# Where a decoder trunk computes its adaLN modulation columns: other quotas for its stages

## The chip, the cores and the metric

The kernel runs on one core of one Trainium2 chip. The metric is the device time of one execution in microseconds. One core has five engines that run their own queues: TensorE (matrix products, here PE; its weight loads are PEld), VectorE (DVE), ScalarE (ACT), GpSimd (POOL) and SyncE (SP), which issues every load of this kernel. Data lies in SBUF, products accumulate in PSUM.

## What is computed

A decoder trunk of four layers over 256 positions and 1,024 features, batch 1. Each layer is a SwiGLU, a token mixer and a second SwiGLU; the mixers are RWKV-7, Mamba-2, sliding-window attention and RWKV-7 again. Each of the twelve sub-layers normalises its input and modulates it by shift, scale and gate vectors that depend on one conditioning vector c:

```python
c_act = jax.nn.silu(c)
for i in range(DEPTH):
    mod = (c_act @ ada_w[i] + ada_b[i]).reshape(bsz, N_SUB, 3, d)
    shift, scale, gate = mod[:, :, 0], mod[:, :, 1], mod[:, :, 2]
    h = adaln(x, norm_g[i, 0], shift[:, 0], scale[:, 0])
    x = x + MACARON_W * gate[:, 0, None] * swiglu(h, ffn_w_in[i, 0], ffn_w_out[i, 0])
    h = adaln(x, norm_g[i, 1], shift[:, 1], scale[:, 1])
    ...
    x = x + gate[:, 1, None] * y
    h = adaln(x, norm_g[i, 2], shift[:, 2], scale[:, 2])
    x = x + MACARON_W * gate[:, 2, None] * swiglu(h, ffn_w_in[i, 1], ffn_w_out[i, 1])
return x
```

The line left out is the mixer. What matters here is the first line of the loop: `c_act @ ada_w[i]` is a vector times a matrix of 1,024 by 9,216 float32 numbers for each layer. None of it depends on x, so it can be computed at any time before the sub-layer that uses it.

## The kernel before

Activations are held transposed, features on the 128 partitions, in eight blocks of 128 x 256. Every dense product is float32 made of three passes on TensorE: a weight tile of 128 x 1,024 floats (512 KB) is loaded by `unit` (lines 292 to 305), ScalarE rounds it to its high half (`whi`, line 299), VectorE subtracts to get the low half (`wlo`, line 303), and then come high x high, high x low and low x high (lines 328 to 330, or 520 to 522 for an output projection). One weight tile is 24 products of 128x128 by 128x256. A SwiGLU has 66 such tiles: 44 of its first matrix, and 22 of its second, whose products are interleaved with the first's as its inputs come.

**Modulation columns.** The modulation is cut into 288 columns of 128 numbers: 72 a layer, 24 a sub-layer (eight pairs of scale and shift, then eight gates). `mod_step` (lines 247 to 262) takes the next of a fixed list, loads its 512 KB of `ada_w` into a buffer named `ada`, and lets VectorE multiply it by c and sum along the row in one instruction (line 253); a small instruction (257 or 261) finishes a scale or a gate. The buffer comes from the same ring of four that the raw weight tiles use (`wp`, tag `raw`), and the load is issued by SP in the order of its queue, between the weight loads.

**Who calls it.** Four mechanisms decide where a column is made:

- A plan (`mod_plan`, 275): a quota of columns spread over a number of weight tiles. After each tile's low half, `mod_tick` (285, called at 304) adds the rate to a credit and makes a column for each whole one, until the quota is used up. A SwiGLU sets its plan from `QUOTA` over 0.8 x 66 = 52.8 tiles (655), so that its last tiles are free of columns; Mamba sets 8 over 48 (871). At the end of either the rate is set to 0, and RWKV and attention set no plan.
- `mod_some(n, upto)` (280): makes up to n columns now, as long as fewer than `upto` have been made in all. RWKV calls it in its recurrence (1561, queued on VectorE behind the end of the triangular inverse), after it beside the bonus terms (1574) and the head reads (1580), and in its output loop `outputs` (1456).
- `mod_until` (264): makes all that is still missing up to a place in the list. It is called where a column is needed: before the residual addition for the gates (545), and in `u_open` or `rw_open` for the scale and shift of the next sub-layer (479, 1053). If enough columns have been made before, it does nothing.
- The first SwiGLU makes its own 16 before it starts.

**The order of the engines.** The code is traced, and the framework puts each engine's instructions into a fixed queue by their dependences and its own estimate of times; `issue_after` pins some behind others. On the chip each engine works through its queue in that order, so an instruction that waits holds up those behind it. At the end of a sub-layer, `out_proj` prefetches up to three weight tiles of the next one, opens its modulation, and then, for each of the eight blocks, finishes the products, adds to x (`x_add`, line 608) and prepares the next input (`u_part`, 490 and 491).

**RWKV.** The stage runs dense products for k, v and r through a queue of pieces (`dense_queue`, `fill`), between which the steps of the decay, the triangular inverse and the recurrence are placed, then `read_heads`, a normalisation for the first four heads (`norm(0)`), the loop `outputs(0, ...)`, a normalisation for the last four heads (`norm(1)`, whose steps are lines 580 to 593 on VectorE, 1081 and 844 on TensorE) and `outputs(1, ...)`. Each turn of the loop gates and splits one block and feeds it to the output projection, which loads one tile of `rwo`.

Of the kernel before, what the change touches and what calls it, by code (L numbers as in the profile page):

```python
# [21 lines left out]
S = 256  # L22
DEPTH = 4

QUOTA = ((24, 28), (28, 28), (28, 24), (24, 0))
DFF = 2816
NJ = D // P
NF = DFF // P
# [155 lines left out]
class Trunk:  # L184
# [465 lines left out]
    def ffn(self, i, s):  # L650
        nc = self.nc
        self.phase(f"ffn{i}{s}")
        with ExitStack() as ctx:
            self.weights(ctx, 7)
            self.mod_plan(QUOTA[i][s // 2], 0.8 * 3 * NF)
            gp1 = ctx.enter_context(self.tc.tile_pool(name="gp1", bufs=1))
# [190 lines left out]
    def mb(self, i, k):  # L847
# [4 lines left out]
        with ExitStack() as ctx:  # L852
# [15 lines left out]
                v.memset(t[:, 0:3], 0.0)  # L868
            tri2 = self.c("tri")[:, None, :].to_broadcast([P, 2, P])

            self.mod_plan(8, 48)
            for g in range(8):
                chans, zs = [], []

# [194 lines left out]
    def rw(self, i, k):  # L1069
# [1 line left out]
        self.phase(f"rw{i}")  # L1071
        v, act = nc.vector, nc.scalar
        hold = [False]
        ahead = 84 if i == 0 else 72 * DEPTH

        def mm(*a, **k):
            ins = nc.tensor.matmul(*a, **k)  # L1077
            self.last = ins.ins if hold[0] else None
# [12 lines left out]
        with ExitStack() as ctx:  # L1091
# [54 lines left out]
            def flat(t):  # L1146
                return t.rearrange("p k c -> p (k c)")
# [271 lines left out]
            def read_heads(g, jj):  # L1419

                s, uv, mr, ys, sn = ss[g], uvs[g], mrs[g], yss[g], sns[:, 16 * g : 16 * g + 16]
                o = self.bank("mm", S)
                for c in range(4):
                    for par, p in enumerate(half):
                        x = o[p, c * 64 : c * 64 + 64]
                        mm(x, uv[:, par, jj, c], mr[:, par, 4 * jj + c], start=True, stop=c == 0)
                        if c:
                            mm(x, s[c - 1][p, jj], er[g][p, jj, c, 1:], start=False, stop=True)
                act.copy(ys[:, jj], o)
                sq = sp.tile([P, S], F32, tag="sq", name="sq")  # L1430
                act.activation(sq, o, AF.Square)
                for b in range(2):
                    mm(sn[:, b * 8 + 2 * jj : b * 8 + 2 * jj + 2], sq[:, b * P : b * P + P], self.c("b2"),
                       start=True, stop=True)
# [6 lines left out]
            def outputs(g, yt, g2, mid):  # L1441
                ys = yss[g]
                oh, ol = (pool.tile([P, 4, S], F32R, tag=f"{t}{g}", name="o") for t in ("b", "e"))
                for jj in range(4):
                    j = 4 * g + jj
                    y = ys[:, jj]
                    rb = self.bank("aux", S)
                    self.heads(rb, 2 * jj, yt)
                    v.scalar_tensor_tensor(y, y, self.v(f"lnw{k}", j), rb, ALU.mult, ALU.mult)
                    v.scalar_tensor_tensor(y, y, self.v(f"lnb{k}", j), kx[g][:, jj], ALU.add, ALU.add)  # L1450
                    o = self.bank("aux", S)
                    mm(o, flat(g2)[:, j * P : j * P + P], sg, start=True, stop=False)
                    mm(o, flat(mid)[0:32, j * P : j * P + P], hm[0:32], start=False, stop=True)
                    v.tensor_tensor(y, y, o, ALU.mult)
                    self.split(oh[:, jj], ol[:, jj], y)
                    self.mod_some(2, ahead)
                    feed(oh[:, jj], ol[:, jj])
                    yield 1

# [66 lines left out]
            def one_by_one(*gens):  # L1526
                gens = list(gens)
                while gens:
                    for x in list(gens):
                        if next(x, 0) == 0:  # L1530
                            gens.remove(x)
                        else:
                            yield
# [22 lines left out]
            more = inner(1, bd)  # L1556
            for n, _ in enumerate(one_by_one(chain(0), chain(1))):
                self.fill()
                if n in range(1, 24, 3):
                    with self.tc.issue_after(self.inv_end):  # L1560
                        self.mod_some(1, ahead)
                if n in (17, 20, 22):
                    self.drain(3 - (17, 20, 22).index(n))
                    next(more)
# [12 lines left out]
            yss[1] = slot("f1", [4, S], "ys")  # L1577
            for jj in range(4):
                read_heads(1, jj)
                self.mod_some(2, ahead)  # L1580
                self.fill(3)
            hold[0] = False
            for _ in outputs(0, yt, g2, mid):
                pass
            for _ in outputs(1, norm(1), g2, mid):
                pass
# [35 lines left out]
```

## Time and profile before

| | |
|---|---|
| three executions | 2573.45, 2555.08 and 2565.6 us; median 2565.6 |
| the profiled execution | 2566.54 us, its span 2564.4 us |
| TensorE clock granted over it | 0.95 of full speed |
| data moved | 521.98 MB, on average 204 GB/s |
| loads of `ada_w` | 288 of 512 KB, median 4.4 us from issue to landing |

The page's strips over 40 slices of 64 us show how the stages differ:

```profile
PE   6999999889999989999999999899999999999999
DVE  7876785788787788988788877997787766866854
PEclk9999997699999998999999999999999998886999
GB/s 312 288 260 154 100 87 145 191 186 298 285 191 293 283 136 123 157 176 186 300 284 190 302 279 155 154 219 290 258 185 295 261 103 74 84 152 179 203 195 128
```

Each digit is the busy share of a slice in tenths, PEclk the granted clock in tenths. TensorE is busy almost throughout. The slices near 300 GB/s are SwiGLUs; those near 100 are RWKV. [...]

### The profile page before, as it was taken

The page shows a single profiled execution, that of the slowest core. Times are in us where ns is not written, and L with a number is a line of the kernel's source. Part 1 is how long each engine was busy: PE and PEld are TensorE (multiplying, and loading weights), DVE is VectorE, ACT ScalarE, POOL GpSimd, SP SyncE. Part 2 cuts the span into 40 slices and gives each one's busy share as a digit, 9 for nine tenths or more (in the row PEclk, how much of TensorE's full clock was granted, in tenths as well). Part 3 has the DMA queues.
Part 4 walks back from the last instruction along what each step waited for, and adds up shares of the span by engine and source line. Part 5 has one row for each costly group of instructions (what it writes and reads, how often), then busy time and mean ns, then how long its engine had stood idle before and what let it go on. Part 6 is the DMA issues. An engine that isn't in the chain of part 4 may idle for free.

```text
span 2564.4 us, 51852 instructions
## 1 busy us (share of the span) xinstructions
PE 2447.3 (95%) x20868; PEld 2280.3 (89%) x20868; DVE 1985.6 (77%) x4181; ACT 1262.2 (49%) x2261; POOL 8.1 (0%) x14
## 2 busy tenths in 40 slices
PE   6999999889999989999999999899999999999999
PEld 5998877689999988999999999799999987777999
DVE  7876785788787788988788877997787766866854
ACT  3446661254454456765445445554454464612643
POOL 0000000000000000000000000000000000000000
PEclk9999997699999998999999999999999998886999
DMA  8874224558858843455885884468758732245663
GB/s 312 288 260 154 100 87 145 191 186 298 285 191 293 283 136 123 157 176 186 300 284 190 302 279 155 154 219 290 258 185 295 261 103 74 84 152 179 203 195 128
DMA packets 145392, 521.98 MB, mean 204 GB/s; under 512 B 16128, under 2 KB 19456, under 8 KB 145024
## 3 DMA queue, kind: packets, MB, share of 16 engines
q1 hardware_dynamic: 145152, 518.67, 60.5%
q8 instruction: 164, 2.69, 0.4%
q14 instruction: 76, 0.62, 0.1%
HBM read 516.50 MB, written 2.10 MB: 202 GB/s over the span
## 4 chain that ended last, share of the span: by engine, by line
PE 55%; DMA 19%; DVE 15%; ACT 5%; issue 4%; ACTq 0%; SPq 0%; DVEq 0%
DMA raw<-ffn 11%; PE aux L1077 8%; DMA ada<-ada_w 7%; PE aux L330 5%; DVE wlo L303 5%; PE aux L328 5%; PE aux L329 5%; PE mm L328 4%; PE mm L329 4%; PE mm L330 4%; PE mm L521 4%; PE mm L520 4%; PE mm L522 4%; ACT whi L299 3%; DVE ada L253 3%
## 5 line engine op out<-in xcount | busy, mean ns | idle before, releaser
L299 ACT CAST whi<-raw 128x1024 fp32r<-128x1024 f32 x671 | 700.1, 1050 | 678.3 <-DMA raw<-ffn 464.8
L303 DVE TENSOR_TENSOR wlo<-raw,whi 128x1024 fp32r<-128x1024 f32 x671 | 817.4, 1222 | 232.1 <-ACT whi L299 225.6
L328 PE MATMUL aux<-hh,whi 128*128 128x256 f32 x2576 | 722.7, 281 | 12.9 <-DVE ft L676 9.8
L330 PE MATMUL aux<-hh,wlo 128*128 128x256 f32 x2576 | 721.4, 280 | 13.3 <-DVE wlo L303 13.2
L329 PE MATMUL aux<-hl,whi 128*128 128x256 f32 x2576 | 719.9, 279 | 0.0
L328 PEld LDWEIGHTS aux<-hh,whi 128*128 128x128 f32 x2576 | 487.1, 189 | 17.8 <-DVE ft L676 12.2
L330 PEld LDWEIGHTS aux<-hh,wlo 128*128 128x128 f32 x2576 | 486.5, 189 | 15.9 <-DVE wlo L303 15.9
L329 PEld LDWEIGHTS aux<-hl,whi 128*128 128x128 f32 x2576 | 489.0, 190 | 0.0
L253 DVE CUSTOM_DVE_ANT_0 ada<-ada,cb,vec 128x1024 f32<-128x1024 f32 x288 | 368.6, 1280 | 88.2 <-DMA ada<-ada_w 88.0
L520 PE MATMUL mm<-gh,whi 128*128 128x256 f32 x1408 | 392.6, 280 | 9.3 <-ACT gh L678 9.3
L522 PE MATMUL mm<-gh,wlo 128*128 128x256 f32 x1408 | 390.4, 280 | 3.3 <-DVE wlo L303 3.1
L521 PE MATMUL mm<-gl,whi 128*128 128x256 f32 x1408 | 392.5, 280 | 0.4
L328 PE MATMUL mm<-hh,whi 128*128 128x256 f32 (+1 forms) x1056 | 313.5, 303 | 13.5 <-ACT cy L885 5.1
L329 PE MATMUL mm<-hl,whi 128*128 128x256 f32 (+1 forms) x1056 | 308.3, 294 | 0.4
L330 PE MATMUL mm<-hh,wlo 128*128 128x256 f32 (+1 forms) x1056 | 307.6, 294 | 0.0
L520 PEld LDWEIGHTS mm<-gh,whi 128*128 128x128 f32 x1408 | 266.1, 189 | 10.9 <-ACT gh L678 10.9
L521 PEld LDWEIGHTS mm<-gl,whi 128*128 128x128 f32 x1408 | 267.0, 190 | 1.8 <-DVE gl L679 1.8
L522 PEld LDWEIGHTS mm<-gh,wlo 128*128 128x128 f32 x1408 | 264.7, 189 | 4.2 <-DVE wlo L303 4.2
L328 PEld LDWEIGHTS mm<-hh,whi 128*128 128x128 f32 x1056 | 205.2, 197 | 28.3 <-issue 7.2
L329 PEld LDWEIGHTS mm<-hl,whi 128*128 128x128 f32 x1056 | 207.6, 197 | 9.1 <-issue 2.5
L330 PEld LDWEIGHTS mm<-hh,wlo 128*128 128x128 f32 x1056 | 207.6, 197 | 5.9 <-issue 4.3
L678 ACT ACTIVATE gh<-ft 128x256 fp32r<-128x256 f32 x176 | 72.9, 415 | 153.1 <-DVE ft L677 152.1
(357 smaller groups left out, 3087.7 us busy)
## 6 DMA issues: line engine op xcount, KB each, us to landing
raw<-ffn SPq DMA_DIRECT2D x522, 512.0 KB, 4.6
ada<-ada_w SPq DMA_DIRECT2D x288, 512.0 KB, 4.4
raw<-rkv SPq DMA_DIRECT2D x48, 512.0 KB, 3.5
raw<-mbin SPq DMA_DIRECT2D x48, 512.0 KB, 3.4
raw<-rwo SPq DMA_DIRECT2D x16, 512.0 KB, 4.5
raw<-mbout SPq DMA_DIRECT2D x16, 512.0 KB, 3.3
lora<-lora SPq DMA_DIRECT2D x12, 512.0 KB, 3.8
raw<-qkv SPq DMA_DIRECT2D x12, 512.0 KB, 4.4
```

Of the source, the lines that this page charges most:

```text
L253: nc.vector.tensor_tensor_reduce(out=raw, in0=raw, in1=self.cb, scale=1.0, scalar=self.v("ada_b", i * 72 + col), op0=ALU.mult, op1=ALU.add ...
L299: nc.scalar.copy(hi[:, :n], raw[:, :n])
L303: nc.vector.tensor_tensor(lo[:, :n], raw[:, :n], hi[:, :n].bitcast(F32), ALU.subtract)
L328: mm(out, hi, xh, start=start, stop=False)
L329: mm(out, hi, xl, start=False, stop=False)
L330: mm(out, lo, xh, start=False, stop=stop)
L520: mm(o, hi, xh, start=k == 0 and j % 2 == 0, stop=False, skip_group_check=True)
L521: mm(o, hi, xl, start=False, stop=False, skip_group_check=True)
L522: mm(o, lo, xh, start=False, stop=k == n - 1 and j % 2 == 1, skip_group_check=True)
L678: nc.scalar.activation(gh, t, AF.Copy, scale=0.5)
L1077: ins = nc.tensor.matmul(*a, **k)
```

## The change

The quotas, two limits and a few calls change; no arithmetic does. All 288 columns are made as before, from the same data with the same instructions, but in other places.

```diff
-QUOTA = ((24, 28), (28, 28), (28, 24), (24, 0))
+QUOTA = ((24, 30), (30, 30), (30, 30), (28, 8))
...
-            self.mod_plan(8, 48)
+            self.mod_plan(14, 48)
...
-        ahead = 84 if i == 0 else 72 * DEPTH
+        ahead = 70 if i == 0 else 280
+        self.mod_plan(10 if i == 0 else 6, 24)
...
                     self.split(oh[:, jj], ol[:, jj], y)
-                    self.mod_some(2, ahead)
                     feed(oh[:, jj], ol[:, jj])
...
-                if n in range(1, 24, 3):
+                if n in range(1, 24, 2 if i == 0 else 3):
                     with self.tc.issue_after(self.inv_end):
                         self.mod_some(1, ahead)
...
                 read_heads(1, jj)
-                self.mod_some(2, ahead)
+                self.mod_some(1, ahead)
                 self.fill(3)
```

In order: the quota of each SwiGLU (first and second of the four layers), Mamba's plan, the limit of `mod_some` in the two RWKV stages and a plan for their dense tiles, which had none, the call in RWKV's output loop taken out, twelve calls instead of eight in the recurrence of layer 0, and one column instead of two at each of the four head reads.

## The prediction

> **What bounds the kernel now.** I read the page first, then the busy times in windows cut at the sub-layers, then the waits and timeline where TensorE stands still.
>
> ```profile
> span 2564.4 us, 51852 instructions
> PE 2447.3 (95%) x20868; PEld 2280.3 (89%) x20868; DVE 1985.6 (77%) x4181; ACT 1262.2 (49%) x2261; POOL 8.1 (0%) x14
> PE 55%; DMA 19%; DVE 15%; ACT 5%; issue 4%; ACTq 0%; SPq 0%; DVEq 0%
> L253 DVE CUSTOM_DVE_ANT_0 ada<-ada,cb,vec 128x1024 f32<-128x1024 f32 x288 | 368.6, 1280 | 88.2 <-DMA ada<-ada_w 88.0
> ```
>
> TensorE is busy for 95% of the span, and the chain that ended last runs more on it than on all else. A modulation column is one 512 KB load and 1.28 us of VectorE; there are 288 before and after. The change moves columns only, so the question is what a column costs in each place. The windows below are the sub-layers: RWKV of layer 0, SwiGLU, SwiGLU, Mamba, SwiGLU, SwiGLU, attention, SwiGLU, SwiGLU, RWKV of layer 3, last SwiGLU.
>
> ```profile
> core 0: us, PE busy (x) PEld busy (x) DVE busy (x) ACT busy (x) POOL busy (x), PEclk, DMA share, GB/s
> 226.50:532.30 305.80, 289.99 (x2744) 233.12 (x2743) 217.57 (x550) 139.98 (x301) 3.50 (x5) 0.84 0.39 130
> 532.30:729.40 197.10, 190.87 (x1602) 189.27 (x1602) 160.87 (x285) 96.47 (x145) 0.00 (x0) 0.99 0.76 254
> 729.40:922.80 193.40, 186.19 (x1595) 183.59 (x1593) 157.54 (x278) 94.96 (x142) 0.00 (x0) 1.00 0.76 254
> 922.80:1176.00 253.20, 246.84 (x1925) 228.48 (x1924) 217.30 (x540) 163.42 (x374) 0.00 (x0) 0.96 0.46 150
> 1176.00:1370.80 194.80, 191.35 (x1601) 189.40 (x1600) 159.36 (x284) 97.19 (x146) 0.00 (x0) 0.99 0.76 254
> 1370.80:1566.40 195.60, 187.42 (x1592) 184.65 (x1592) 158.01 (x281) 94.23 (x142) 0.00 (x0) 0.99 0.76 254
> 1566.40:1677.30 110.90, 97.00 (x751) 87.56 (x750) 101.03 (x398) 60.76 (x164) 0.00 (x0) 0.92 0.47 158
> 1677.30:1869.00 191.70, 187.24 (x1594) 185.83 (x1592) 152.71 (x268) 95.57 (x142) 0.00 (x0) 1.00 0.76 249
> 1869.00:2061.90 192.90, 188.78 (x1580) 187.57 (x1579) 151.96 (x262) 93.82 (x140) 0.45 (x1) 0.99 0.74 247
> 2061.90:2379.00 317.10, 302.45 (x2786) 238.87 (x2785) 220.28 (x564) 141.14 (x301) 3.52 (x5) 0.84 0.36 119
> 2379.00:2564.40 185.40, 180.26 (x1574) 179.46 (x1572) 118.51 (x191) 86.72 (x128) 0.00 (x0) 1.00 0.55 177
> ```
>
> The first column is the stage's time, the second TensorE's. Attention idles most for its length (14 us of 111); both RWKV stages have a granted clock of 0.84. The columns in seven of the same windows:
>
> ```profile
> 226.50:532.30 305.80, 45.95 (x36) 0.84 0.39 130
> 532.30:729.40 197.10, 35.87 (x28) 0.99 0.76 254
> 922.80:1176.00 253.20, 8.97 (x7) 0.96 0.46 150
> 1566.40:1677.30 110.90, 16.51 (x13) 0.92 0.47 158
> 1677.30:1869.00 191.70, 30.77 (x24) 1.00 0.76 249
> 2061.90:2379.00 317.10, 40.91 (x32) 0.84 0.36 119
> 2379.00:2564.40 185.40, 0.00 (x0) 1.00 0.55 177
> ```
>
> **Counting the columns.** The order of columns is fixed, so running the new quotas through the code gives the new places. Three SwiGLU quotas of 28 that follow each other, and a fourth, become 30 (8 columns more in all); 24 becomes 30 behind attention (6) and 28 ahead of the last RWKV (4). Mamba has 46 of its 48 planned loads inside the plan, so 14/48 gives 13 instead of 7 (6). Attention has no quota: it makes whatever is missing up to column 208 in one burst. It starts with 195 and needs 13 now; it will start with 203 and need 5. RWKV 0 goes from 36 to 30: some 7 beside the dense products, 13 in the recurrence instead of 8, 8 instead of 12 after it, 2 in the output loop instead of 16. RWKV 3 goes from 32 to 15: about 5 beside dense products, 8 in the recurrence as before, and the limit of 280 leaves one or two after it. The last SwiGLU makes 7. So 31 columns leave attention (8) and RWKV (6, 17), and 25 go to SwiGLUs and 6 to Mamba.
>
> **Attention: -10.** Here the burst stands between the residual additions, in VectorE's queue, while TensorE's next products are queued behind the additions and wait for them.
>
> ```profile
> L253 DVE CUSTOM_DVE_ANT_0 ada<-ada,cb,vec 128x1024 f32<-128x1024 f32 x10 | 12.7, 1283 | 1.3 <-DMA ada<-ada_w 1.3
> L520 PE MATMUL mm<-oh,whi 128*128 128x256 f32 x12 | 5.3, 445 | 10.6 <-DVE x L608 10.6
> 1656.00:1676.00 20.00, 9.38 (x47) 8.60 (x46) 18.66 (x45) 5.18 (x14) 0.00 (x0) 0.66 0.83 293
> ```
>
> These are the groups and the window of 1656 to 1676: ten columns (12.7 us), 10.6 us of idle TensorE behind them, and a clock of 0.66, so that 2 x 0.34 x 20 = 13.6 us went by at half speed with TensorE half busy. Eight columns fewer leave five. Three of the 13 ran before 1656, so by the old times two of the five remain, 2.6 us: 10.6 - 2.6 = 8 us of waiting goes, and I estimate 2 us of the slow products. Late next are those two. Bounds: -6 (the five stand where the ten stood, half the wait stays) to -13 (all of it, with the clock).
>
> **The output loops: -13.** In RWKV 0 TensorE runs through its first four heads' output without a break, then waits for the second normalisation, whose short VectorE steps are queued between columns. In RWKV 3 the same place waits less:
>
> ```profile
> 499.96 0.38 PE L1081 MATMUL aux<-con,ry 128*8 128x128 f32 x2 [2.79 <-DVE ry L593]
> 502.05 0.58 PE L844 MATMUL aux<-yth,hot 8*128 8x256 f32 x1 [1.70 <-ACT yth L835]
> ```
>
> ```profile
> 2348.69 0.38 PE L1081 MATMUL aux<-con,ry 128*8 128x128 f32 x2 [0.93 <-DVE ry L593]
> 2350.18 0.41 PE L844 MATMUL aux<-yth,hot 8*128 8x256 f32 x1 [1.11 <-ACT yth L835]
> ```
>
> ```profile
> 502.00:526.00 24.00, 22.95 (x108) 18.04 (x108) 17.29 (x33) 5.72 (x8) 0.00 (x0) 0.68 0.57 188
> 2348.00:2373.00 25.00, 23.20 (x116) 18.08 (x116) 14.18 (x31) 8.13 (x14) 0.00 (x0) 0.73 0.40 138
> ```
>
> The waits are 4.5 and 2.0 us; without columns the steps are ready while TensorE still works on the first four heads, and I count 4 and 1.5 us as gone. What follows is bound by TensorE (22.95 of 24 us, 23.20 of 25) at clocks of 0.68 and 0.73: 2 x 0.32 x 24 = 15.4 and 2 x 0.27 x 25 = 13.5 us at half speed, worth 7.7 and 6.7 us if the clock stayed up. I take half, 7.2, as the stages' mean of 0.84 shows that the clock falls elsewhere too: 4 + 1.5 + 7.2, about 13. Bounds 0 (the rwo load or its split is late instead) to 21. [...]
>
> The four columns fewer in the head reads of each stage count nothing: TensorE works without a break there.
>
> **Columns beside the dense products and in the recurrence: +5.** Seventeen new places (7 and 5, and 4 or 5 in RWKV 3), and each puts a load into SP's queue and the ring of four raw buffers that it shares with the weights, and 1.28 us into VectorE's queue, behind which stand the chain's own steps and the next weight's split; TensorE waits for those. POOL's fills wait for none of it.
>
> ```profile
> 290.00:320.00 30.00, 30.00 (x353) 25.57 (x351) 23.58 (x68) 20.69 (x48) 0.95 (x1) 0.96 0.29 98
> 400.00:420.00 20.00, 18.59 (x260) 15.21 (x259) 13.68 (x34) 3.89 (x9) 0.00 (x0) 1.00 0.49 159
> ```
>
> In the first window (dense products) TensorE never stops and DMA is at 0.29, in the second (recurrence, with six columns in 20 us) it stops for 1.4 us. So the cover is the dense queue. Bounds 0 and 17 x 1.28 = 22; I take 0.3 us each, near the row with six columns and 1.4 us.
>
> **Mamba: +2.** Six columns, 7.7 us of VectorE, in a stage where it is busy for 217 of 253 us and TensorE for 247. Bounds 0 and 7.7; a quarter, since TensorE's queue covers most.
>
> **SwiGLUs: +12.** With 24 columns they took 191.7 and 192.9, with 28 they took 193.4, 194.8 and 195.6 (leaving out 197.1, which begins behind RWKV): 2.3 us for 4 columns, 0.58 each. The last took 185.4 with none, so from none to 24 a column is 0.29. New: 8 + 6 + 4 = 18 at 0.58 is 10.4, and 7 at 0.29 is 2.0. The bounds come from these windows inside the SwiGLUs, and the last one from a stretch where TensorE has run out of weights:
>
> ```profile
> 1230.00:1290.00 60.00, 60.00 (x512) 60.00 (x511) 47.91 (x72) 27.04 (x34) 0.00 (x0) 1.00 0.89 301
> 2420.00:2480.00 60.00, 60.00 (x532) 60.00 (x531) 37.53 (x47) 29.12 (x39) 0.00 (x0) 1.00 0.68 220
> 842.00:882.00 40.00, 36.62 (x305) 35.71 (x305) 29.36 (x48) 17.43 (x24) 0.00 (x0) 1.00 0.83 277
> ```
>
> TensorE has two rhythms without any idle time: 60/512 = 117 ns a product and 60/532 = 113. A weight tile is 24 products, 2.81 or 2.71 us, and a quota of 30 in 52.8 tiles asks for 1.568 loads of 0.524 MB in it: 293 GB/s in the slow rhythm, 304 in the fast. The loads reach 301. So in the slow rhythm 18 columns cost nothing (bound 0), in the fast one they make TensorE wait, as at 842, at 0.524/301 = 1.74 us a load (bound 18 x 1.74 = 31). I take the difference between the stages, which lies between. [...]
>
> **Sum.** -10 - 13 + 5 + 2 + 12 = -4 (rounded from -3.6) against the profiled execution of 2566.5 us, whose span is 2564.4: 2563 us. That execution is 1 us above the median of the three runs, 2565.6. A measurement of this kernel tells about 1% (26 us) from no change; the three runs alone are 18 us apart.
>
> **The rivals.**
>
> *The loads become the bound (slower).* Place: the seven SwiGLUs. Price: 1.74 us for each of 25 columns, 43.5 instead of 12.4. It decides once TensorE is in the fast rhythm, 304 asked against 301 reached. Time: 2563 + 31 = 2594. For it: the waits at 842. Against it: the slow rhythm covers, and the last SwiGLU has DMA at 0.68.
>
> *The SwiGLUs cover their columns and the clock stays up (faster).* Place: 502 to 526 and 2348 to 2373, and the SwiGLUs in the slow rhythm. Output loops -20, attention -13, SwiGLUs +2, Mamba and dense products +5: -26, 2540. For it: at 28 columns 512 products in 60 us with no idle time. Against it: the stages with 28 are longer than those with 24. [...]
>
> *The change doesn't do what it says.* If the list scheduling leaves the remaining attention columns and output-loop loads where they block now, both gains halve: 2563 + 11 = 2574.
>
> *The rhythm.* 66 x 24 = 1,584 products a SwiGLU at 4.4 ns is 7 us, and each pause of TensorE seems to choose anew; eight SwiGLUs can shift the time by some 10 us either way without any reason in the change.
>
> **How the numbers follow.** Forecast and its neighbourhood 0.60, covered and warm 0.17, loads the bound 0.09, gains halved 0.14. Faster than 2540: most of the second, 0.17. Slower than 2591: most of the third, 0.08. Within 1%: 0.75. The range takes in attention's and the loops' bounds on one side and the loads' on the other, without their ends: 2534 to 2590.
>
> **What would show it.** Right: 5 columns in attention and TensorE's idle time before its last products under 4 us; attention near 101 us; no wait of 2.8 us for the second normalisation; SwiGLUs of 193 to 198 us; a last SwiGLU of 186 to 189. Wrong: idle TensorE in the SwiGLUs above 10 us each with SP waiting for VectorE, new waits in RWKV before its recurrence, or a granted clock in RWKV under 0.84.

## The result and the profile after

The changed kernel takes 2584.7 us (median of seven executions, 2578.9 to 2599.4) against 2565.6 us for the kernel before (seven, 2554.4 to 2573.5): a ratio of 1.0101, with a 95% interval of 1.0071 to 1.0130. The time lies in the range of 2534 to 2590, because that range took in a bound for slower loads; the forecast itself was 4 us less, and the kernel became 19 us slower. The profiled execution took 2583.94 us, 17.4 more than that of before. Its page begins so:

```profile
span 2582.2 us, 51802 instructions
PE 2435.1 (94%) x20868; PEld 2265.3 (88%) x20868; DVE 1983.3 (77%) x4181; ACT 1261.5 (49%) x2261; POOL 8.1 (0%) x14
PE 41%; DMA 27%; DVE 19%; ACT 7%; issue 5%; ACTq 0%; SPq 0%; DVEq 0%
```

The chain that ended last tells it first: TensorE's share fell from 55% to 41%, the loads' rose from 19% to 27% and VectorE's from 15% to 19%. TensorE is busy for 12 us less in a span that is 18 us longer, so 30 us of new idle time stand in it. The windows by sub-layer say where (columns as before: stage, its time, TensorE and its products, weight loads, VectorE, ScalarE, POOL, clock, DMA share, GB/s):

```profile
0.00:235.30 235.30, 198.13 (x1548) 191.32 (x1549) 171.47 (x299) 98.25 (x149) 0.71 (x5) 0.98 0.78 267
235.30:540.90 305.60, 283.67 (x2755) 228.84 (x2754) 208.53 (x532) 139.34 (x300) 3.46 (x5) 0.84 0.35 118
540.90:740.40 199.50, 187.74 (x1592) 184.71 (x1591) 162.91 (x290) 97.20 (x147) 0.00 (x0) 0.98 0.76 256
740.40:939.90 199.50, 189.30 (x1593) 185.85 (x1592) 160.03 (x283) 94.66 (x142) 0.00 (x0) 0.99 0.75 252
939.90:1199.50 259.60, 248.02 (x1925) 229.38 (x1925) 224.50 (x557) 163.26 (x373) 0.00 (x0) 0.96 0.49 159
1199.50:1396.90 197.40, 189.06 (x1603) 185.70 (x1602) 162.09 (x289) 96.54 (x146) 0.00 (x0) 1.00 0.76 256
1396.90:1595.50 198.60, 189.30 (x1594) 185.88 (x1593) 160.16 (x283) 94.01 (x142) 0.00 (x0) 0.99 0.76 256
1595.50:1693.70 98.20, 93.33 (x752) 84.35 (x752) 89.86 (x376) 60.17 (x162) 0.00 (x0) 0.98 0.41 135
1693.70:1893.00 199.30, 189.49 (x1590) 186.47 (x1589) 161.15 (x289) 95.33 (x144) 0.00 (x0) 0.98 0.77 255
1893.00:2088.00 195.00, 190.46 (x1581) 189.04 (x1581) 157.21 (x273) 94.30 (x140) 0.38 (x1) 0.98 0.76 256
2088.00:2395.10 307.10, 295.05 (x2787) 232.84 (x2786) 198.69 (x515) 141.02 (x301) 3.58 (x5) 0.87 0.29 94
2395.10:2582.20 187.10, 181.50 (x1573) 180.91 (x1571) 126.70 (x211) 87.41 (x127) 0.00 (x0) 0.99 0.60 195
```

The first window was not shown of the kernel before; there it reads:

```profile
0.00:226.50 226.50, 198.86 (x1548) 192.53 (x1549) 170.45 (x296) 97.98 (x149) 0.67 (x5) 0.99 0.80 275
```

Against the prediction's terms, stage by stage in the two profiled executions:

| stage | predicted | measured |
|---|---|---|
| first SwiGLU (quota 24 as before) | 0 | +8.8 |
| the seven later SwiGLUs | +12 | +25.5 |
| Mamba | +2 | +6.4 |
| attention | -10 | -12.7 |
| RWKV 0 and 3 (loops -13, the rest +5) | -8 | -10.2 (-0.2 and -10.0) |
| sum | -4 | +17.8 |

The two gains came as forecast or better. The three costs came to 41 us instead of 14. The experiments ask what each of them is.

### The profile page after: what moved, and what is told of

It is laid out like the page before. It is cut to its first block, busy times and chain, and to the rows that moved or that the text cites. A ratio compares the mean times of both kernels' runs of the same rounds, so it can differ in the third digit from the quotient of the medians.

```text
span 2582.2 us, 51802 instructions
## 1 busy us (share of the span) xinstructions
PE 2435.1 (94%) x20868; PEld 2265.3 (88%) x20868; DVE 1983.3 (77%) x4181; ACT 1261.5 (49%) x2261; POOL 8.1 (0%) x14
## 4 chain that ended last, share of the span: by engine, by line
PE 41%; DMA 27%; DVE 19%; ACT 7%; issue 5%; ACTq 0%; SPq 0%; DVEq 0%
DMA raw<-ffn 19%; PE aux L1078 8%; DVE wlo L303 8%; DMA ada<-ada_w 7%; ACT whi L299 5%; PE mm L328 4%; PE mm L329 4%; PE mm L330 4%; DVE ada L253 4%; PE mm L1078 3%; PE mm L521 3%; PE mm L520 3%; PE mm L522 3%; PE aux L330 2%; PE aux L328 2%
## 5 line engine op out<-in xcount | busy, mean ns | idle before, releaser
L330 PEld LDWEIGHTS aux<-hh,wlo 128*128 128x128 f32 x2576 | 489.2, 190 | 27.1 <-DVE wlo L303 26.7
```

Of the source, the lines that this page charges most:

```text
L330: mm(out, lo, xh, start=False, stop=stop)
```

## The experiments

Each ratio is to the kernel before on the same chip. In diffs, lines with - are those of the changed kernel, unless the kernel before is named.

**The first SwiGLU.** Nothing in it was changed, yet it is 8.8 us longer. These are the end of it in VectorE's timeline, SP's and TensorE's (start, duration, engine, line, operation; in brackets the idle time before and what ended it):

```profile
219.30 0.42 DVE L677 TENSOR_TENSOR ft<-ft,aux 128x256 f32<-128x256 f32 x1
223.59 1.28 DVE L253 CUSTOM_DVE_ANT_0 ada<-ada,cb,vec 128x1024 f32<-128x1024 f32 x1 [3.87 <-DMA ada<-ada_w]
224.80 0.08 DVE L253 DVE_READ_ACCUMULATOR2_ANT mod<- 128x1 f32 x1
224.80 0.42 DVE L679 SCALAR_TENSOR_TENSOR gl<-ft,gh 128x256 fp32r<-128x256 f32 x1
```

```profile
218.89 0.33 SPq L252 DMA_DIRECT2D ada<-ada_w  x1
```

```profile
220.23 0.58 PE L520 MATMUL mm<-gh,whi 128*128 128x256 f32 x1 [3.08 <-ACT gh L678]
225.28 0.58 PE L521 MATMUL mm<-gl,whi 128*128 128x256 f32 x1 [4.47 <-DVE mod L261]
```

The first column of RWKV 0's new plan has been drawn ahead of `gl`, the last step that TensorE's final products need. SP's queue shows how it came there: six loads of RWKV's weights stand ahead of it, the three that the SwiGLU prefetches and three of RWKV's own code, which the framework's order has drawn into this phase together with the column that hangs on the third of them. SP could issue its load only at 218.89, VectorE waits 3.87 us for it, and TensorE waits 4.47 us behind VectorE. That is half of the 8.8 us; the granted clock is also lower afterwards, 0.70 from 220.2 us to the end of the stage against 0.88 over the last 14.5 us before, and the rest was not followed. The edit holds the planned columns back until the next sub-layer's input exists:

```diff
+        self.pin = self.last_dg
...
-            self.mod_step()
+            with ExitStack() as c:
+                if self.pin is not None:
+                    c.enter_context(self.tc.issue_after(self.pin))
+                self.mod_step()
```

> The changed kernel, with RWKV's planned columns held behind the normalisation at the start of RWKV on VectorE; nothing else. Theory (a column of RWKV's plan stands in VectorE's queue ahead of the first SwiGLU's last low half, and TensorE waits for its load): the first SwiGLU falls from 235 us to 227 to 230, the idle 4.5 us before its last output products goes, and the time falls by 5 to 9 us, to about 2578. Rival (those 9 us are chance in the loads of that stage): 235 us again, within 4 us of 2585.

Measured: 2575.7 us, ratio 1.0060 (1.0028 to 1.0092), its interval overlapping that of the change. The stage itself is plain, in its window and in the groups of its last 23 us:

```profile
0.00:227.90 227.90, 196.09 (x1548) 189.46 (x1549) 170.63 (x296) 98.22 (x149) 0.68 (x5) 0.99 0.80 274
```

```profile
L524 PE MATMUL mm<-gl,whi 128*128 128x256 f32 x32 | 9.8, 305 | 0.6 <-DVE gl L682 0.6
```

The wait before the `gl` products is 0.6 us. With the plan and the shared ring the stage took 232.9 to 235.3 us in five kernels of this study; with the shared ring and nothing drawn ahead it took 226.5 to 228.8 in four. So a single column of 1.28 us, drawn ahead into this place, costs some 6 us. Most of that hangs on the late load: in the kernel below that gives the columns buffers of their own, the same column is drawn ahead as well, VectorE waits 2.4 us for its load, and TensorE 1.1 us behind it.

**The columns in the SwiGLUs.** Six of them went from a mean of 194.3 us with 26.7 columns to 198.2 with 29.7: 1.32 us a column, where the prediction had 0.58. (Three other kernels of this study with the same quotas give 197.5, 197.5 and 196.2, so 0.6 to 1.1.) Over the seven, 20.8 of the 25.5 us are new idle time of TensorE (38.8 to 59.6). To find the price by itself, three kernels keep the stages and vary the quota and Mamba's plan. In them nothing is forced at the ends of stages, attention has no columns, and where the list of columns runs out it starts again. First none:

```diff
-QUOTA = ((24, 30), (30, 30), (30, 30), (28, 8))
+QUOTA = ((24, 0), (0, 0), (0, 0), (0, 0))
...
-            self.mod_plan(14, 48)
+            self.mod_plan(0, 48)
```

> The changed kernel with no columns in the seven later SwiGLUs and in Mamba, none forced at the ends of stages, and none after the recurrence in the last RWKV; modulation that isn't computed is left at 0.5. Theory (each column adds load time): SwiGLUs of 181 to 185 us with TensorE idle for 3 to 5 us, Mamba about 250, attention about 95. Rival (SwiGLUs differ by TensorE's two rhythms and by their starts, not by columns): some of the seven still at 190 or more.

Measured: 2488.3 us, ratio 0.9724 (0.9684 to 0.9763). Then 24 in each, and 8 in Mamba's plan:

```diff
+QUOTA = ((24, 24), (24, 24), (24, 24), (24, 24))
...
+            self.mod_plan(8, 48)
```

> As the kernel without columns, with 24 in each of the seven later SwiGLUs and 8 planned in Mamba; modulation that isn't computed is left at 0.5. Theory (each column adds load time, more of it the closer the loads are to their limit): mean of the seven 190 to 193 us, Mamba 253. Rival (columns are covered up to some number between 24 and 30): 184 to 187.

Measured: 2550.6 us, ratio 0.9969 (0.9944 to 0.9995). And 36 in each, 20 in Mamba's plan:

```diff
+QUOTA = ((24, 36), (36, 36), (36, 36), (36, 36))
...
+            self.mod_plan(20, 48)
```

> As the kernel with 24 columns in each of the seven later SwiGLUs, with 36 in each and 20 planned in Mamba, in the shared ring of four. Theory (over some 24 to 28 columns the ring is the bound and each further one costs a load's time, 1.0 to 1.8 us): the seven take 203 to 213 us on average, Mamba 263 to 268. Rival (the price stays at the 0.4 us a column that lies between none and 24): 196 to 198, Mamba 255.

Measured: 2679.1 us, ratio 1.0427 (1.0304 to 1.0550). The seven SwiGLUs took 182.6, 191.8 and 208.3 us on average, TensorE idle for 0.8, 4.9 and 14.2 us in each. (The last one is taken up to its last addition to x.) A column costs 0.38 us up to 24 and 1.37 us from 24 to 36. The price rises: the kernels with 30 columns lie between, at 0.8 to 1.2 us a column from 24 to 30 and 1.7 to 2 from 30 to 36, so whether there is a kink or a steady bend is not shown. One SwiGLU, the first of layer 2, by its windows with 0, 24 and 36 columns:

```profile
1351.20:1533.60 182.40, 182.30 (x1594) 181.74 (x1593) 123.49 (x206) 94.47 (x142) 0.00 (x0) 1.00 0.57 192
```

```profile
1377.90:1568.00 190.10, 188.58 (x1595) 187.88 (x1594) 153.19 (x270) 94.39 (x142) 0.00 (x0) 1.00 0.75 251
```

```profile
1441.40:1647.20 205.80, 192.68 (x1595) 187.00 (x1594) 167.91 (x300) 95.84 (x142) 0.00 (x0) 0.99 0.78 262
```

The same 1,594 products fill 182, 189 and 193 us of TensorE. The 189 are the slow rhythm that the prediction read from the kernel before. In the middle of this stage, with no and with 24 columns, TensorE is busy throughout at full clock, and runs 885 products in 100 us or 851:

```profile
1400.00:1500.00 100.00, 100.00 (x885) 100.00 (x884) 58.16 (x74) 46.03 (x61) 0.00 (x0) 1.00 0.59 196
1430.00:1530.00 100.00, 100.00 (x851) 100.00 (x850) 76.84 (x118) 44.64 (x59) 0.00 (x0) 1.00 0.84 282
```

A stage that runs in the slow rhythm from end to end is some 7 us longer. With 24 columns two of the seven did, with none and with 36 no stage did; so the 0.38 is in part the rhythm, and the price above 24 is not. What sets the rhythm is open.

**What the price is made of.** The rival of the prediction has the transfers at their limit. The other theory is the ring: a column holds one of the four `raw` buffers that the weights use, until VectorE has read it, and SP can issue no further load meanwhile. In the middle of a SwiGLU of the changed kernel the waits are these (engine, line, what it waited for: us, times, longest):

```profile
ACT whi L299 <- DMA raw<-ffn: 62.5, 34, 3.8
DVE wlo L303 <- ACT whi L299: 22.0, 23, 2.1
PEld aux L328 <- DVE ft L676: 3.0, 3, 2.6
PEld aux L330 <- DVE wlo L303: 2.5, 4, 0.9
```

ScalarE waits for weights, VectorE for ScalarE, TensorE for VectorE. SP, which issues the loads, waits at the column's load (line 252) for a buffer that VectorE's `wlo` frees:

```profile
SPq L252 <- DVE wlo L303: 17.6, 13, 2.4
```

To part transfer from buffer, the columns of the SwiGLUs get two buffers of their own, with nothing else changed in the code:

```diff
-        raw = self.wp.tile([P, D], F32, tag="raw", name="ada")
+        raw = (self.ap or self.wp).tile([P, D], F32, tag="raw" if self.ap is None else "adaf", name="ada")
...
+            if self.layers[i][0] != "x":
+                self.ap = ctx.enter_context(self.tc.tile_pool(name="ap", bufs=2))
+                ctx.callback(setattr, self, "ap", None)
```

> The changed kernel, with two buffers of their own for the columns made in SwiGLUs; the weights keep the ring of four. Theory (the ring of four that columns and weights share sets the rate of the loads in a SwiGLU with 30 columns): the six SwiGLUs with 28 or 30 columns lose 3 to 6 us each, TensorE's idle time in them falls from 4 to 12 us to under 5, time 2550 to 2567. Rival (the transfers themselves are at their limit near 300 GB/s): each within 2 us of the changed kernel's, time 2577 to 2593.

Measured: 2532.3 us, ratio 0.9902 (0.9867 to 0.9938), a larger gain than either theory had. The seven later SwiGLUs fell by 43 us together, but unevenly: the first of them not at all (201.0 us, 11.9 of them idle), the next by 11.6. The columns also move when they have their own buffers: the six make 38, 22, 37, 23, 30 and 28 instead of 30, 30, 30, 30, 30 and 28. The middle of a SwiGLU, first in the changed kernel and then with the ring of its own:

```profile
1430.00:1550.00 120.00, 115.04 (x973) 113.42 (x972) 93.56 (x146) 51.37 (x67) 0.00 (x0) 0.99 0.86 288
```

```profile
1700.00:1800.00 100.00, 100.00 (x885) 100.00 (x884) 90.14 (x144) 49.31 (x62) 0.00 (x0) 1.00 0.94 344
```

With six buffers the loads run at 344 GB/s and TensorE never stops; with four they run at 288 while TensorE waits. So the transfers were not at their limit, the buffers were. Over 100 us of a later SwiGLU, no kernel with the ring of four moved more than 303 GB/s. The prediction had read its 301 as the transfers' limit. A shorter stretch of the same SwiGLU moves 360:

```profile
1698.00:1758.00 60.00, 60.00 (x531) 60.00 (x531) 56.98 (x89) 32.35 (x42) 0.00 (x0) 1.00 0.97 360
```

Whether it is the separate ring or the number of six that helps was not told apart: six shared buffers were not tried.

The same edit on the kernel before asks whether the change itself is then worth anything:

> The kernel before, with two buffers of their own for the columns made in SwiGLUs. Theory (the shared ring of four is near its limit with 28 columns already, and over it with 30): the SwiGLUs with 24 and 28 columns lose 3 to 8 us each, time 2530 to 2545; with the limit gone in both, the changed kernel with its own ring (2532) is no longer the slower one. Rival (the ring binds only at 30): SwiGLUs within 2 us of before, time 2558 to 2570.

Measured: 2532.5 us, ratio 0.9895 (0.9855 to 0.9934), as the theory had it. With the own ring the two quotas can't be told apart: the ratios are 0.9902 and 0.9895, with intervals of 0.4% (10 us) to either side. Where a column has its own buffer, no gain or loss of the change shows.

**Attention's burst and the output loops.** From the kernel before, eight columns of attention's burst and the 16 and 12 columns of the loops are left out (their modulation is a constant), and nothing is put elsewhere:

```diff
+        del self.todo[-8:]
...
-                    self.mod_some(2, ahead)
+                    for _ in range(2):
+                        if len(self.todo) > 72 * DEPTH - ahead:
+                            self.todo.pop()
```

> The kernel before, with eight columns of attention's burst and the columns of RWKV's output loops (16 and 12) left out, their modulation left at 0.5; nothing is made elsewhere instead. Theory (they stood in TensorE's way there): attention falls from 111 to 98 us, RWKV 0 by 12 to 16 us, RWKV 3 by 8 to 12, time 2525 to 2535. Rival (attention's burst is real, the output loops' gain in the changed kernel was the clock's chance): attention 98, RWKV within 4 us of before, time 2550 to 2556.

Measured: 2549.3 us, ratio 0.9961 (0.9934 to 0.9987). Attention falls to 98.3 us, as in the changed kernel. The RWKV stages lose only 3.8 and 3.7 us (302.0 and 313.4 against 305.8 and 317.1). So the rival came closer than the theory. The window from the head reads on, in RWKV 0, first before and then without the loop's columns, with two stretches of the latter:

```profile
474.60:532.30 57.70, 49.40 (x252) 39.42 (x252) 47.74 (x107) 18.08 (x32) 0.00 (x0) 0.74 0.67 219
```

```profile
477.00:530.60 53.60, 51.68 (x257) 41.24 (x257) 28.96 (x63) 16.24 (x29) 0.00 (x0) 0.69 0.24 85
```

```profile
440.00:470.00 30.00, 30.00 (x154) 21.23 (x153) 7.91 (x22) 2.63 (x8) 0.00 (x0) 0.50 0.31 106
480.00:500.00 20.00, 20.00 (x50) 12.38 (x50) 9.61 (x25) 2.69 (x7) 0.00 (x0) 0.50 0.01 2
```

Six us of idle time go here (8.3 to 1.9); over the whole stage it is 3.4 (15.8 to 12.4), since the wait for the first normalisation, just ahead of this window, is now 3.6 us instead of 1.1. In RWKV 3 the idle time doesn't fall (14.6 to 15.1). The clock moves within the stage. These are the last 58 us in two parts, first before and then without the loop's columns:

```profile
474.30:502.30 28.00, 23.51 (x123) 18.44 (x123) 25.02 (x60) 6.71 (x10) 0.00 (x0) 0.74 0.81 266
502.30:532.30 30.00, 26.19 (x130) 21.09 (x131) 23.02 (x49) 11.67 (x22) 0.00 (x0) 0.73 0.53 173
```

```profile
472.60:500.60 28.00, 24.75 (x62) 15.12 (x63) 16.28 (x48) 4.14 (x10) 0.00 (x0) 0.50 0.16 56
500.60:530.60 30.00, 28.08 (x199) 26.55 (x199) 17.07 (x31) 13.55 (x22) 0.00 (x0) 0.84 0.35 123
```

In the last 30 us, where the prediction looked, the clock rises from 0.73 to 0.84, but in the 28 us ahead of them it falls from 0.74 to 0.50, and over the stage it stays at 0.84. For 30 us ahead of the loop (440 to 470) and from 480 to 500 it is at 0.50, with TensorE busy throughout by its records. So the low clock of the stage is there without the loop's columns too.

**Columns beside RWKV's dense products.** From the changed kernel the plan of the RWKV stages is taken out; its columns are made after the recurrence instead:

```diff
-        self.mod_plan(10 if i == 0 else 6, 24)
...
-                self.mod_some(1, ahead)
+                self.mod_some(2 if i == 0 else 1, ahead)
...
-                self.mod_some(1, ahead)
+                self.mod_some(3 if i == 0 else 1, ahead)
```

> The changed kernel without the plan in RWKV: its ten columns of layer 0 are made beside the bonus terms and the head reads (2 and 3 a turn, up to the same 70), those of layer 3 one a turn there. Theory (each column beside the dense products of RWKV 0 costs more than its 1.28 us, one after the recurrence costs nothing, and without a plan no column is drawn ahead into the first SwiGLU): RWKV 0 falls from 306 to 294 to 300 us, the first SwiGLU to 227 to 230, time 2562 to 2574. Rival (the loads after the recurrence now delay the output projection's weights): RWKV 0 306 or more.

Measured: 2562.9 us, ratio 1.0015 (0.9987 to 1.0043), an interval below that of the change. The first SwiGLU is back at 228.8 us, and RWKV 0 is 11.7 us shorter:

```profile
228.80:522.70 293.90, 281.86 (x2755) 226.28 (x2754) 210.15 (x535) 139.79 (x300) 3.47 (x5) 0.87 0.36 125
```

With the plan, TensorE waits for three steps of VectorE's chains up to the recurrence: first the waits of the changed kernel from 236 to 380 us, then those from 380 to 460.

```profile
PE aux L1078 <- DVE bk L1239: 2.9, 1, 2.9
```

```profile
PE aux L1078 <- DVE o L1281: 3.8, 1, 3.8
PE aux L1078 <- DVE g L1305: 3.4, 2, 2.7
```

Without it, the same steps cost 0.3, 0 and 0.8 us: 9 us of the difference. In the second stretch the kernel without the plan has more column work on VectorE than the one with it (27.2 us against 22.9), which points to the columns ahead of that stretch. How each step came to be late behind them was not followed further.

TensorE's idle time in RWKV 0 is the surer measure: 15.8 us before, 21.9 with the plan (21.8 to 22.0 in seven kernels with it), 12.0 without, and 12.4 in the kernel before without the loop's columns. The stage's time moves more between executions than these differences: it took 304.9 to 313.6 us in those seven, at clocks of 0.84 down to 0.81. So the 0 that the stage table shows for RWKV 0 hides some 10 us of idle time added by the plan. In RWKV 3 the plan adds 1 us (12.0 against 11.0). By the same reading RWKV 3 took 299.1 to 311.1 us (mean 308.3) in seven kernels with the plan, and 317.1 and 319.9 in two with the old columns; its gain of 10 stands.

**Mamba.** The 13 columns are loaded as before, but VectorE does not multiply and sum them (their modulation is a constant):

```diff
+        if self.skip:
+            return
```

> The changed kernel with Mamba's 13 columns loaded but not computed: VectorE skips them there, their modulation stays at 0.5. If VectorE's 1.28 us each are what Mamba pays for (it is busy for 87% of that stage): Mamba falls from 260 to 252 to 254 us. If it is the place that the loads take in the ring: 257 or more.

Measured: 2573.1 us, ratio 1.0036 (0.9999 to 1.0072). Mamba's windows, with 13 loads and no VectorE work, and then with 19 whole columns in the kernel of 36:

```profile
934.40:1184.60 250.20, 246.11 (x1928) 227.66 (x1928) 209.41 (x522) 162.60 (x373) 0.00 (x0) 0.97 0.48 165
```

```profile
957.50:1231.60 274.10, 258.70 (x1927) 236.97 (x1926) 231.72 (x571) 164.68 (x373) 0.00 (x0) 0.93 0.47 160
```

With none the stage took 252.4 us, with 7 it took 253.2, with 13 259.6, with 19 274.1: six columns cost 6.4 us on top of seven, and the next six 14.5. The loads alone cost nothing; what Mamba pays for comes with the work on VectorE, on which its own chain runs too. Two things stay open: a load whose column is not computed has no reader on VectorE that holds its buffer, so the run takes away that hold as well, and the last six columns cost 2.4 us each, more than their 1.28 us on VectorE.

**Together.** The own ring, no RWKV plan, Mamba's old quota, and what that leaves over in the SwiGLUs, which can now carry it:

```diff
-QUOTA = ((24, 30), (30, 30), (30, 30), (28, 8))
+QUOTA = ((24, 34), (34, 34), (36, 30), (30, 8))
...
-            self.mod_plan(14, 48)
+            self.mod_plan(8, 48)
```

> The changed kernel with two buffers of their own for the columns in SwiGLUs, no plan in RWKV (as in the run without it), Mamba's plan back at 8, and quotas of 34, 34, 34, 36, 30, 30 and 8 in the later SwiGLUs. Theory (columns in SwiGLUs are nearly free once they leave the weights' ring; those in Mamba and beside RWKV's dense products are not): against 2532 with its own ring alone, Mamba 6 us, RWKV 0 6 to 12 us and the first SwiGLU 0 to 5 us shorter, time 2508 to 2520. Rival (34 columns overload the transfers in the SwiGLUs): SwiGLUs of 195 us and more, time 2530 to 2545.

Measured: 2499.6 us (2491.5 to 2511.2), ratio 0.9757 (0.9714 to 0.9800): it beats both kernels and what was expected of it. In its profile, the slowest of its four executions (2511.2 us), four of the seven later SwiGLUs run in the slow rhythm and take 193 to 197 us, and the three in the fast one 182 to 188, whatever their columns. The SwiGLU of layer 2 with 36 columns, which took 205.8 us in the shared ring:

```profile
1351.20:1536.90 185.70, 183.00 (x1594) 182.01 (x1593) 165.50 (x301) 94.84 (x142) 0.00 (x0) 1.00 0.80 285
```

## Why the prediction was wrong

*What bounds the kernel, and the count.* Right: TensorE, with the loads next. The new places of the columns came out as counted: 5 in attention, 13 in Mamba, 7 in the last SwiGLU, 15 in RWKV 3, and 29 in RWKV 0, whose thirtieth was drawn ahead into the first SwiGLU.

*Attention, -10.* Right in mechanism and nearly in size: -12.7, near the bound that also takes in the clock, which rose from 0.92 to 0.98. Of it, 9.0 us are idle time (13.9 to 4.9), where 8 were counted. The half speed that goes into the bound is in the trace of before: the granted clock was 0.50 from 1661 to 1674 us, and 1.00 from 1657 to 1660. These are the groups of 1677 to 1697 us, around its end at 1693.7:

```profile
L253 DVE CUSTOM_DVE_ANT_0 ada<-ada,cb,vec 128x1024 f32<-128x1024 f32 x5 | 6.2, 1280 | 0.0
L520 PE MATMUL mm<-oh,whi 128*128 128x256 f32 x24 | 5.9, 299 | 1.7 <-DVE x L608 1.7
```

All five columns stand there, not two, as the prediction had it, and yet TensorE waits 1.7 us instead of 10.6.

*The output loops, -13.* Half right on the waits, wrong on the clock, which was 0.50 from 503 to 517 us before; that it would stay up without the columns was an estimate, which no row of before shows. The wait for the second normalisation goes in both stages, but in RWKV 0 the one for the first grows to 3.5 us; leaving out the loop's columns alone took 3.4 us of idle time from RWKV 0 and none from RWKV 3, where 5.5 were counted. The clock rose in the 30 us that the prediction looked at, and fell in the 28 us ahead of them, so the 7.2 us were not there in RWKV 0. The RWKV stages still sum to -10.2 against -8 forecast, but by two errors against each other, which is luck: RWKV 0 gained nothing, and RWKV 3 gained 10, more than its loop gives. Of those 10 us, 7.4 are busy time of TensorE, at a clock of 0.87 against 0.84 (0.85 to 0.89 in the seven kernels with the plan); what raises it there is open.

*Columns beside the dense products and in the recurrence, +5.* Too small. The plan's seven in RWKV 0 alone added some 10 us of idle TensorE, about 1.4 us each, over the upper bound (1.28 us each) and not the 0.3 taken; in RWKV 3 they added 1. The prediction took the price from a stretch of the recurrence; it had no row with columns beside dense products.

*The first SwiGLU, nothing.* A step that was missing: the framework's order draws the first weight tiles of RWKV into the last phase of the SwiGLU ahead of it, and a column that the plan hangs on one of them comes along, in VectorE's queue before `gl`. The price was 8.8 us in this pair and 7.4 of it came back with the pin.

*Mamba, +2.* Mis-sized: 6.4. A quarter of VectorE's time was assumed on the path; it was 0.83 of it (6.4 of 7.7).

*SwiGLUs, +12.* The largest miss, and the step that decides: 25.5 in this pair (21, 21 and 19 in the three other kernels with the same quotas). Of the signs of a failure that the prediction listed, it is the first, though not as strong as written: six SwiGLUs with 4.5 to 11.8 us of idle TensorE, two of them above 10, and SP waiting for VectorE. The prediction read a slope of 0.58 from 24 to 28 columns and carried it on to 30. The stages of before differed in more than their columns, and between 24 and 36 the price is 1.37. Behind it stands the wrong limit: the 301 GB/s were taken for what the transfers can do, and the ring of four, which the prediction named only beside RWKV's columns, was left out of this term. The last SwiGLU, +1.7 for seven columns, came as forecast (2.0).

*The rivals.* The one on the other side, the loads as the bound, was right in place and in direction: 25.5 of its 43.5. It was wrong on what is short. What had looked like the limit of the transfers was that of the buffers: at most 303 GB/s over 100 us with four, 344 with two more. *Covered and warm* failed: the SwiGLUs cost 25.5 instead of 2, and the RWKV stages gave 10.2 instead of 20. (Its sum takes Mamba and the dense products as +5, where the prediction's own terms give +7.) *The rhythm* is real and of the size given, some 7 us a SwiGLU: the last one took 187 us with seven columns in the four kernels in which it ran fast, and 193.2 and 195.6 with eight in the two in which it ran slow. Seven executions of the changed kernel lie 20 us apart; whether the rhythm makes that spread is not shown. It doesn't explain the sign here: the seven SwiGLUs together were longer in each of the four kernels with these quotas and the shared ring, all but one of the changed kernel's ran mostly in the fast rhythm, and 20.8 of its 25.5 us are recorded idle time.

## What to carry to other kernels

A side job that costs little at 24 a stage need not cost little at 30 (here 0.38 us a column up to 24 and 1.37 from 24 to 36): measure its price at two quotas around the one wanted before moving more of it in. Where a side job borrows buffers from the ring that feeds the main work, give it its own first; here that was worth 1%, and the move of the columns alone cost 1%. And when a plan hangs items on the first loads of a loop, look whether those loads are drawn ahead into the stage before: the item then lands there too, ahead of whatever closes that stage.

## What was unexpected

- Transfers: with 512 KB loads and a ring of four no 100 us of a later SwiGLU moved more than 303 GB/s; with two more buffers for the columns it was 344, and 360 over 60 us, with TensorE busy throughout.
- The granted clock was 0.50 from 480 to 500 us in the kernel without the loop's columns, and from 440 to 470, though TensorE's records leave no gap there. What holds it down is open.
- Busy time doesn't tell how well TensorE is fed: 1,594 products of the same shape took 182.3 us of it with no columns, 188.6 with 24, in the slow rhythm, and 192.7 with 36, beside 13 us of idle time. A whole stage can run at 113 or at 118 ns a product, at full clock either way.
